# Attention scores in split precision: the second pass on half the rows of TensorE, two of them beside each other

## The chip, the cores and the metric

The kernel runs on one core of a Trainium2 chip. The metric is the device time of one execution in microseconds (us), as the median of several runs. Engines are called as in the profile: PE is TensorE's matmul, PEld its weight load, DVE VectorE, ACT ScalarE, POOL GpSimd, and SP SyncE, which here issues DMAs.

## What is computed

One layer of a hybrid encoder over 1024 prompt frames and 32 sample frames, all in float32: a combined projection, an attention branch and a convolution branch that are merged by gates, an output projection, an MLP, a gated embedding and norms. The change touches the attention of the prompt: 8 heads of width 64, 128 queries at a time, no softmax.

```python
def stick_breaking(q, k, v, q_pos, k_pos):
    scale = 1.0 / math.sqrt(HEAD_DIM)
    z = jnp.einsum('bqhd,bkhd->bhqk', q.astype(jnp.float32), k.astype(jnp.float32)) * scale
    mask = k_pos[None, :] < q_pos[:, None]
    log_1m = jnp.where(mask, jax.nn.log_sigmoid(-z), 0.0)
    tail = lax.cumsum(log_1m, axis=3, reverse=True) - log_1m
    a = jnp.where(mask, jnp.exp(jax.nn.log_sigmoid(z) + tail), 0.0)
    out = jnp.einsum('bhqk,bkhd->bqhd', a, v.astype(jnp.float32))
```

## The kernel before

Matmuls are done in split precision: a float32 operand becomes a high part in TensorE's rounded format and a low part, the rest; a product then takes two or three matmuls, high by high, high by low and low by high, added up in PSUM.

The attention is written as 64 steps (p, j, i): 4 pairs of heads (p), 2 heads in each (j), 8 query blocks (i). Step i looks at L = 128(i + 1) keys. The work of one step is spread over the program's next ones: `scores` in step n (matmuls into a PSUM tile z, a sigmoid on ACT into r, a causal select on POOL), `weigh` in step n+1 (a scan on DVE), `flip` in step n+2 (transposes pa on PE, cast on ACT and subtraction on DVE into at), and after each second block `gather` (the matmuls av against the values, which ACT and DVE take out and add). The string `ORDER = "LSAFBFG"` sets the order inside a step: scan, scores, transposes, fill (F), further transposes, fill, gather.

Fill is other work for PE, in units of a few hundred ns: the embedding projection (ps_pw, ps_pt) and the output of the convolution branch (ps_oc). `pace` spreads it: it estimates what the chain of a step needs (`load`) and what PE does for the step itself (`own`), and gives each step a share of the fill. The order on PE, DVE, ACT and POOL is the order in which the code is written; DMAs from SP stand in the order in which the tile framework schedules them.

A head is 64 wide, and PE's array has 128 rows. So the tile `kk` (ks in the profile) holds a head's high part of the keys in rows 0 to 63 and the low part in rows 64 to 127. The tile `q` has two versions of the queries: `q[:, 0]` with the high part above and the low part below, `q[:, 1]` the other way round. The first pass (L1206) gives high by high plus low by low, the second (L1207) the two mixed products, each for 128 queries and W keys. W is L up to 512 keys; from 640 keys on there are two z tiles of W = L/2 (320 to 512), one after the other. A pool of two PSUM buffers holds them.

`keys_values` fetches the keys and the values of a head by SP, eight steps before its step of index 2 (six before its first). All its tiles come from one pool of 37 blocks (`blk`), which other work uses too.

The 32 sample frames have an attention of their own in the same stretch (tiles zs, pas, avs). Its matmuls use parts of the array: zs (L1450) 64 rows and 32 columns, avs 128 rows and 64 columns (L1481) and 32 rows and 64 columns (L1483). The profile writes this as rows*columns.

Of the kernel before, what the change touches and what calls it, by code (L numbers as in the profile page):

```python
# [9 lines left out]
F32 = mybir.dt.float32  # L10
F32R = mybir.dt.float32r
# [4 lines left out]
P = 128  # L16
D = 1024
KD = D // P
SEQ = 1024
# [47 lines left out]
START = 0.33  # L67
BP = (8, 9)
TAIL = 0
FILL = 23.28 - START - TAIL  # L70
MM = {mybir.EngineType.Activation, mybir.EngineType.PE, mybir.EngineType.DVE, mybir.EngineType.Pool}

# [2 lines left out]
def tile_step(  # L75
# [8 lines left out]
    nc = tc.nc  # L84
# [7 lines left out]
    def blk(name, dt=F32, shape=None):  # L92
        return bpool.tile(shape or [P, T], dt, tag="B", name=name)
# [705 lines left out]
    kd = dpool.tile([4, 2, P, SEQ], F32, name="kd")  # L799
# [36 lines left out]
    st, cst = {}, {}  # L836
# [336 lines left out]
    def keys_values(p, j):  # L1173
        kk = st["k", p, j] = blk(f"ks{p}{j}", F32R, [P, SEQ])
        for i in range(2):
            nc.sync.dma_start(kk[64 * i : 64 * i + 64, :].bitcast(F32), kd[p, i, 64 * j : 64 * j + 64, :])
        vv = st["v", p, j] = blk(f"vv{p}{j}", F32R, [P, 8, P])
        nc.sync.dma_start(vv.bitcast(F32).rearrange("p a c -> p (a c)"), vd[p, j])

# [17 lines left out]
    def scores(p, j, i):  # L1197
        q, kk = live["q", p, j, i // 2], st["k", p, j]
        L = P * (i + 1)
        nh = 1 if L <= 512 else 2  # L1200
        W = L // nh
        tq = slice((i % 2) * P, (i % 2) * P + P)
        r = apool.tile([P, SEQ], F32, tag="R", name=f"r{p}{j}{i}", bufs=4)
        for h in range(nh):
            z, c = zps.tile([P, 512], F32, tag="z", name=f"z{p}{j}{i}{h}")[:, :W], slice(h * W, h * W + W)
            nc.tensor.matmul(z, q[:, 0, tq], kk[:, c], start=True, stop=False)  # L1206
            nc.tensor.matmul(z, q[:, 1, tq], kk[:, c], start=False, stop=True)  # L1207
            nc.scalar.activation(r[:, c], z, AF.Sigmoid, scale=-1.0)  # L1208
        earlier(r[:, L - P : L], 1.0)
        live[p, j, i] = (r, L)  # L1210

    def earlier(a, fill):

        n = a.shape[-1]
        nc.gpsimd.affine_select(  # L1215
            a, a, pattern=[[-1, n]], compare_op=ALU.is_gt, fill=fill, base=0, channel_multiplier=1
        )
# [170 lines left out]
    with tc.manual_schedule(engines=MM):  # L1388
# [17 lines left out]
        for a in range(3, last_, 2):  # L1406
# [4 lines left out]
            run(input_pair(a, a + 1))  # L1411
        m = blk(f"m1_i{last_}"), blk(f"m2_i{last_}")
        side.append(after(2, call(p_fetch), call(keys_values, 0, 0), call(queries, 0, 0, 0), call(queries, 0, 0, 1), call(queries, 0, 0, 2), call(queries, 0, 0, 3)))
        side.append(after(8, *(call(p_parts, f) for f in range(2)), *(call(embed_weights, i) for i in range(2))))
        side.append(after(9, call(next, work)))
# [9 lines left out]
    zps = c_att.enter_context(tc.tile_pool(name="zps", bufs=2, space=PSUM))  # L1425
# [63 lines left out]
    def pace():  # L1489

        ns = len(steps)

        def size(n):
            return steps[n][2] + 1 if 0 <= n < ns else 0

        load, own = [], []
        for n in range(ns + LAG):
            a, b, c = size(n - 1), size(n - LAG), size(n - LAG - 1)
            v = 0.29 * a + 0.17 * b + 0.35 + 0.42 * (c % 2 == 0 and c > 0)
            load.append(max(v, 1.6) + 3.0 * (n == 6 + 4) + 0.5 * (n == 4 + 4) + 0 * (n > 16 and n % 16 in BP))  # L1500
            own.append(0.24 * size(n) + 0.11 * b + 0.24 * c * (c % 2 == 0))
        for more in (None,):
            unit = (FILL * 2.92 + sum(own)) / sum(load)
            part = [max(0.0, unit * v - o) for v, o in zip(load, own)]
            part = [x * FILL / sum(part) for x in part]
            ends = [sum(part[: n + 1]) for n in range(ns + LAG)]
            if more is not None:
                load[next(n for n, e in enumerate(ends) if e > more)] += 0
        return ends

    sample = samples()
    nf = ORDER.count("F")
    pace_ = [0.0] + pace()
    with tc.manual_schedule(engines=MM):
        next(sample)
        for n in range(len(steps) + LAG + 1):
            done_f, parts = 0, None
            w0, w1 = (pace_ + [FILL])[n : n + 2]
            if n < len(steps):
                i = steps[n][2]  # L1520
                if i % 2 == 0 and 4 <= n < len(steps) - 4:
                    p_, j_, i_ = steps[n + 4]
                    queries(p_, j_, i_ // 2)
                if i == 2 and n + 8 < len(steps):
                    keys_values(*steps[n + 8][:2])
# [3 lines left out]
            for op in ORDER:  # L1529
                if op == "S" and n < len(steps):  # L1530
                    scores(*steps[n])
                elif op == "L":
                    if 1 <= n <= len(steps):
                        weigh(*steps[n - 1])
                    settle_owed()
                elif op == "F":
                    done_f += 1
                    fill(START + w0 + (w1 - w0) * done_f / nf)
                elif op == "G" and n > LAG and steps[n - LAG - 1][2] % 2 == 1:
                    p, j, i_ = steps[n - LAG - 1]  # L1540
                    gather(p, j, i_ // 2)
                elif op in "AB" and LAG <= n < len(steps) + LAG:
                    if op == "A":
                        parts = flip(*steps[n - LAG])
                    next(parts, None)
# [1010 lines left out]
```

## Time and profile before

| | |
|---|---|
| median of 3 runs | 1513.21 us (1512.92 to 1514.24) |
| span of the profiled execution | 1512.7 us |
| PE busy in the span | 1494.0 us (99%) |
| chain that ended last | PE 91%, DVE 5%, ACT 2%, issue 1%, DMA 1% |
| first to last score matmul | 430.8 to 600.0 us |
| DMA queue of SP and others (q1) | 260.44 MB, 51.0% of 16 engines |

The profile gives the span alone for its execution; the median of the runs is 0.5 us above it. The span runs from the first instruction recorded to the last. Matmul durations in the records overlap, since the array is filled by one while another drains; how far apart their starts or ends are says more than their length. The chain of waits follows the work that ended last back through what released each instruction, so the time beside an entry is what it added.

### The profile page before, as it was taken

What the parts mean: (1) busy time and instruction counts of PE and PEld (TensorE: products, weight loads), DVE (VectorE), ACT (ScalarE), POOL (GpSimd) and SP (SyncE); (2) the same over time, 40 slices, a digit from 0 to 9 for tenths busy, and PEclk for the clock granted to TensorE, in tenths of its full rate; (3) what the DMA queues carried; (4) which work ended last, traced back from release to release, by engine and by line L of the source; (5) the groups of instructions that cost most, each with busy time, mean ns of one, the idle gap of its engine ahead of it and who ended that gap; (6) DMA issues with size and microseconds to landing.
All of it is one profiled execution on the core that took longest, in us unless ns stands there. A gap on an engine that the chain in (4) does not pass through costs nothing.

```text
span 1512.7 us, 29442 instructions
## 1 busy us (share of the span) xinstructions
PE 1494.0 (99%) x11552; PEld 1479.0 (98%) x11552; DVE 1152.1 (76%) x1624; ACT 791.1 (52%) x1567; POOL 376.1 (25%) x334
## 2 busy tenths in 40 slices
PE   8999999999999999999999999999999999999997
PEld 8999999999999999999999999999999999999997
DVE  7667689779668999886786676666688878879766
ACT  6654444444467667433475545555555433334655
POOL 1234335444121232003324434333000000000251
PEclk9999999999999999999999999999999999999999
DMA  6624424422679676654644334444879757855443
GB/s 231 207 90 170 148 69 182 158 93 100 211 249 284 178 172 139 228 199 152 231 166 147 139 136 156 157 150 157 303 287 279 255 185 231 301 189 165 142 129 123
DMA packets 116747, 275.52 MB, mean 182 GB/s; under 512 B 14048, under 2 KB 30048, under 8 KB 116608
## 3 DMA queue, kind: packets, MB, share of 16 engines
q1 hardware_dynamic: 112720, 260.44, 51.0%
q0 software_dynamic: 1728, 6.29, 2.5%
q10 hardware_dynamic: 2160, 6.91, 1.4%
q8 instruction: 91, 1.49, 0.4%
q14 instruction: 48, 0.39, 0.1%
HBM read 196.10 MB, written 85.88 MB: 186 GB/s over the span
## 4 chain that ended last, share of the span: by engine, by line
PE 91%; DVE 5%; ACT 2%; issue 1%; DMA 1%; SPq 0%; ACTq 0%; DVEq 0%
PE ps_dn L1996 6%; PE ps_dn L1995 6%; PE ps_dn L1994 6%; PE ps_A11i L370 4%; PE ps_A11u L371 4%; PE ps_A11i L371 4%; PE ps_A11u L370 4%; PE ps_A11u L372 4%; PE ps_A11i L372 4%; PE av L1277 3%; PE ps_wo L132 2%; PE ps_wo L133 2%; PE ps_wo L134 2%; PE ps_S1i L372 2%; PE ps_S1i L371 2%; PE ps_S1i L370 2%
## 5 line engine op out<-in xcount | busy, mean ns | idle before, releaser
L1996 PE MATMUL ps_dn<-fhP,wlo_dn 128*128 128x264 f32 x768 | 218.6, 285 | 0.0
L1995 PE MATMUL ps_dn<-flP,whi_dn 128*128 128x264 f32 x768 | 218.2, 284 | 0.2 <-DVE flP L1860 0.2
L1994 PE MATMUL ps_dn<-fhP,whi_dn 128*128 128x264 f32 x768 | 218.3, 284 | 0.0
L1995 PEld LDWEIGHTS ps_dn<-flP,whi_dn 128*128 128x128 f32 x768 | 144.5, 188 | 0.4 <-DVE flP L1860 0.4
L1996 PEld LDWEIGHTS ps_dn<-fhP,wlo_dn 128*128 128x128 f32 x768 | 144.5, 188 | 0.2 <-DVE wlo_dn L1844 0.2
L1994 PEld LDWEIGHTS ps_dn<-fhP,whi_dn 128*128 128x128 f32 x768 | 144.5, 188 | 0.0
L1222 DVE TENSOR_TENSOR_SCAN r<-r 128x128 f32<-128x128 f32 (+3 forms) x64 | 86.7, 1355 | 5.3 <-POOL r L1215 5.3
L2209 POOL TENSOR_TENSOR xx<-xx,pgs 128x400 f32<-128x400 f32 (+1 forms) x17 | 20.1, 1184 | 280.9 <-DVE pgs L2208 280.9
L370 PE MATMUL ps_A11i<-T,shS_i 128*128 128x264 f32 x288 | 82.7, 287 | 1.0 <-ACT u_i L514 1.0
L372 PE MATMUL ps_A11i<-T,slS_i 128*128 128x264 f32 x288 | 81.8, 284 | 0.5 <-DVE slS_i L249 0.5
L371 PE MATMUL ps_A11i<-T,shS_i 128*128 128x264 f32 x288 | 82.1, 285 | 0.0
L370 PE MATMUL ps_A11u<-T,shS_u 128*128 128x264 f32 x256 | 73.3, 286 | 0.0
L371 PE MATMUL ps_A11u<-T,shS_u 128*128 128x264 f32 x256 | 73.0, 285 | 0.0
L372 PE MATMUL ps_A11u<-T,slS_u 128*128 128x264 f32 x256 | 72.7, 284 | 0.0
L1215 POOL TENSOR_SCALAR_AFFINE_SELECT r<-r 128x128 f32<-128x128 f32 x64 | 35.7, 559 | 131.9 <-ACT r L1208 131.8
L1838 ACT CAST whi_dn<-raw_dn 128x1024 fp32r<-128x1024 f32 x31 | 32.6, 1051 | 64.8 <-PE ps_dn L1995 52.7
L1860 DVE TENSOR_TENSOR flP<-mrP,fhP 128x1056 fp32r<-128x1056 f32 x48 | 59.9, 1250 | 4.9 <-ACT fhP L1855 4.8
L134 PE MATMUL ps_wo<-mh,wlo_wo 128*128 128x352 f32 x192 | 62.0, 323 | 0.0
L133 PE MATMUL ps_wo<-ml,whi_wo 128*128 128x352 f32 x192 | 62.0, 323 | 0.0
L132 PE MATMUL ps_wo<-mh,whi_wo 128*128 128x352 f32 x192 | 61.7, 324 | 0.0
L249 DVE TENSOR_TENSOR slS_i<-s_i,shS_i 128x512 fp32r<-128x512 f32 x54 | 48.9, 905 | 12.7 <-ACT shS_i L190 12.4
L1262 DVE TENSOR_TENSOR at<-pa,at 128x512 fp32r<-128x512 f32 (+2 forms) x96 | 50.4, 547 | 9.4 <-ACT at L1261 8.6
(1702 smaller groups left out, 5793.1 us busy)
## 6 DMA issues: line engine op xcount, KB each, us to landing
raw_dn<-in_w_down_dram SPq DMA_DIRECT2D x59, 512.0 KB, 5.6
mrP<-mdT SPq DMA_DIRECT2D x32, 528.0 KB, 5.8
mdB<-m SPq DMA_DIRECT2D x48, 264.0 KB, 2.1
mrP<-mdB SPq DMA_DIRECT2D x24, 528.0 KB, 6.6
s<-gd SPq DMA_DIRECT2D x16, 528.0 KB, 5.3
mdT<-ta SPq DMA_DIRECT2D x32, 264.0 KB, 3.1
raw_pg<-in_w_ple_gate_dram SPq DMA_DIRECT2D x15, 512.0 KB, 3.5
gd<-m_i SPq DMA_DIRECT2D x12, 528.0 KB, 3.0
```

What stands on the lines that cost most here:

```text
L132: nc.tensor.matmul(ps, wh, xh[k][:, cols], start=(k == order[0]), stop=False)
L133: nc.tensor.matmul(ps, wh, xl[k][:, cols], start=False, stop=False)
L134: nc.tensor.matmul(ps, wl, xh[k][:, cols], start=False, stop=(k == order[-1]))
L370: nc.tensor.matmul(p_, wh[:, k, :], h, start=new and n == 0, stop=False, **on)
L371: nc.tensor.matmul(p_, wh[:, k, :], l, start=False, stop=False, **on)
L372: nc.tensor.matmul(p_, wl[:, k, :], h, start=False, stop=z, **on)
L1222: nc.vector.tensor_tensor_scan(rev, rev, rev, 1.0, ALU.mult, ALU.bypass)
L1262: nc.vector.tensor_tensor(al, pt[:, :nb, :], ah.bitcast(F32), op=ALU.subtract)
L1860: dve(l, mraw.pop(v), opd[v].bitcast(F32), op=sub)
L1994: nc.tensor.matmul(ps, hi[:, j, :], oh, start=j == 0, stop=False)
L1995: nc.tensor.matmul(ps, hi[:, j, :], ol, start=False, stop=False)
L1996: nc.tensor.matmul(ps, lo[:, j, :], oh, start=False, stop=j == NP_ - 1)
```

## The change

- `keys_values` writes the high part of the keys into both halves of `kk`, and a second tile `kl` (`low`) gets the low part: keys 0 to 511 in rows 0 to 63, keys 320 to 1023 in rows 64 to 127. That is two DMAs more for each head.
- `scores` makes one pass with all 128 rows for each z tile: `q[:, 0]` against the high part twice gives high by high plus low by high. Then comes one pass with 64 rows for each z tile, the high part of the queries against the low part of the keys. From 640 keys on there are two of these, the first in rows 0 to 63, the second in rows 64 to 127, on different rows and into different z tiles. The product of the two low parts is no longer computed.
- Steps with up to 512 keys have one pass with 128 rows and one with rows 0 to 63.
- Both z tiles are taken before the first sigmoid; the sigmoids stand behind all matmuls of the step.
- `pace` gives steps with 640 keys and more a smaller `own`.

```diff
+FAR = 320
...
         for i in range(2):
-            nc.sync.dma_start(kk[64 * i : 64 * i + 64, :].bitcast(F32), kd[p, i, 64 * j : 64 * j + 64, :])
+            nc.sync.dma_start(kk[64 * i : 64 * i + 64, :].bitcast(F32), kd[p, 0, 64 * j : 64 * j + 64, :])
+        low = st["l", p, j] = blk(f"kl{p}{j}", F32R, [P, SEQ - FAR])
+        for i, c in enumerate((slice(0, SEQ // 2), slice(FAR, SEQ))):
+            nc.sync.dma_start(
+                low[64 * i : 64 * i + 64, : c.stop - c.start].bitcast(F32), kd[p, 1, 64 * j : 64 * j + 64, c]
+            )
...
-        for h in range(nh):
-            z, c = zps.tile([P, 512], F32, tag="z", name=f"z{p}{j}{i}{h}")[:, :W], slice(h * W, h * W + W)
-            nc.tensor.matmul(z, q[:, 0, tq], kk[:, c], start=True, stop=False)
-            nc.tensor.matmul(z, q[:, 1, tq], kk[:, c], start=False, stop=True)
+        low = st["l", p, j]
+        zs_, cs_ = [], [slice(h * W, h * W + W) for h in range(nh)]
+        for h, c in enumerate(cs_):
+            zs_.append(zps.tile([P, 512], F32, tag="z", name=f"z{p}{j}{i}{h}")[:, :W])
+            nc.tensor.matmul(zs_[h], q[:, 0, tq], kk[:, c], start=True, stop=False)
+        for h, c in enumerate(cs_):
+            rows_, n0 = slice(64 * h, 64 * h + 64), c.start - h * FAR
+            nc.tensor.matmul(zs_[h], q[rows_, h, tq], low[rows_, n0 : n0 + W], start=False, stop=True)
+        for z, c in zip(zs_, cs_):
             nc.scalar.activation(r[:, c], z, AF.Sigmoid, scale=-1.0)
...
-            own.append(0.24 * size(n) + 0.11 * b + 0.24 * c * (c % 2 == 0))
+            own.append((0.24 - 0.028 * (size(n) > 4)) * size(n) + 0.11 * b + 0.24 * c * (c % 2 == 0))
```

Two places show what it does to the order. On PE, in the first head, from the transposes (pa) of the step with 512 keys to those of the next, which has 640; z are the two score tiles, ps_pw is fill. Before:

```order
L1258 MATMUL pa_5652<-ident,r_5598 128x128 x2
L1134 MATMUL ps_pw_5657<-p0h,pw0h 128x352
L1135 MATMUL ps_pw_5657<-p0l,pw0h 128x352
L1136 MATMUL ps_pw_5657<-p0h,pw0l 128x352
L1134 MATMUL ps_pw_5657<-p1h,pw0h 128x352
L1135 MATMUL ps_pw_5657<-p1l,pw0h 128x352
L1136 MATMUL ps_pw_5657<-p1h,pw0l 128x352
L1206 MATMUL z_5672<-ks_5348,q_5407 128x320
L1207 MATMUL z_5672<-ks_5348,q_5407 128x320
L1206 MATMUL z_5676<-ks_5348,q_5407 128x320
L1207 MATMUL z_5676<-ks_5348,q_5407 128x320
L1258 MATMUL pa_5685<-ident,r_5621 128x128 x3
```

On PE at the same place after the change (kl are the low halves, 64 rows each; the lines are those of the changed kernel):

```order
L1269 MATMUL pa_5658<-ident,r_5601 128x128 x2
L1214 MATMUL z_5669<-ks_5348,q_5410 128x320
L1214 MATMUL z_5671<-ks_5348,q_5410 128x320
L1217 MATMUL z_5669<-kl_5351,q_5410 128x320
L1217 MATMUL z_5671<-kl_5351,q_5410 128x320
L1269 MATMUL pa_5682<-ident,r_5627 128x128 x3
L1135 MATMUL ps_pw_5688<-p0h,pw0h 128x352
L1136 MATMUL ps_pw_5688<-p0l,pw0h 128x352
```

The two passes against ks now stand together, the two against kl behind them, and a block of six fill matmuls has moved from ahead of the scores to behind the transposes.

On SP, the loads of the third head's keys and values (q are queries, ed an output of the fill). Before:

```order
L1169 DMA q_5980<-qd 64x2x256
L1170 DMA q_5980<-qd 64x256
L1171 DMA q_5980<-qd 64x256
L1176 DMA ks_5984<-kd 64x1024 x2
L1178 DMA vv_5987<-vd 128x1024
L1139 DMA ed<-em_5964 128x1056
```

On SP after the change:

```order
L1171 DMA q_5986<-qd 64x256
L1172 DMA q_5986<-qd 64x256
L1177 DMA ks_5990<-kd 64x1024 x2
L1180 DMA kl_5993<-kd 64x512
L1180 DMA kl_5993<-kd 64x704
L1184 DMA vv_5996<-vd 128x1024
L1140 DMA ed<-em_5970 128x1056
```

The two loads of kl stand between the high halves and the values; what follows keeps its order.

## The prediction

> **What bounds the kernel now.** First the page: TensorE is busy from end to end at the full granted clock. Then the stretch that the edit touches, the 64 attention steps, by the view of windows (us, then busy time and count of each engine, granted clock, DMA share, GB/s).
>
> ```profile
> PE 1494.0 (99%) x11552; PEld 1479.0 (98%) x11552; DVE 1152.1 (76%) x1624; ACT 791.1 (52%) x1567; POOL 376.1 (25%) x334
> PEclk9999999999999999999999999999999999999999
> ...
> 430.60:601.20 170.60, 168.58 (x1215) 159.16 (x1214) 147.49 (x201) 122.92 (x322) 45.26 (x87) 1.00 0.75 207
> ```
>
> TensorE has 2 us of gaps in 170.6; VectorE is busy 147.5 and has 23 to spare. So time that TensorE gains or loses here moves the end, unless it falls into one of its few waits. The waits of this stretch, TensorE's (and its weight loader's) alone (us in total, times, the longest):
>
> ```profile
> PEld pa L1258 <- PE z L1207: 1.5, 4, 0.4
> PEld av L1277 <- DVE at L1262: 1.4, 3, 0.5
> PEld z L1206 <- ACT r L1208: 0.9, 2, 0.5
> PE av L1277 <- DVE at L1262: 0.8, 3, 0.3
> PEld avs L1481 <- issue: 0.4, 2, 0.3
> PE z L1206 <- ACT r L1208: 0.4, 2, 0.2
> ```
>
> The first, second and fourth (3.7 us, at three or four places) are the handovers between heads, where VectorE and ScalarE are late. Busy times of matmuls overlap, so what a pass costs I read from the chain of waits, in order of time (start, time added, what), where each matmul adds only what it lengthens:
>
> ```profile
> 171.15 0.11 PE pts_v L923
> 171.26 0.12 PE ps_A11i L370
> ...
> 446.67 1.00 PE zs L1450 x16
> 447.67 0.26 PE z L1206
> 447.92 0.11 PE z L1207
> ...
> 455.38 0.18 PE z L1207
> ...
> 461.92 0.15 PE z L1207
> ...
> 468.67 0.93 PE av L1277 x8
> 469.61 0.36 PE avs L1481 x8
> 469.97 0.23 PE avs L1483 x4
> 470.20 0.43 PE z L1206
> 470.63 0.23 PE z L1207
> ...
> 472.91 0.18 PE ps_pw L1136
> ...
> 532.17 0.21 PE z L1207
> ```
>
> A score pass over 320, 384, 448 and 512 keys adds 0.15, 0.18, 0.21 and 0.23 us. And the row that decides this case: at 470.20 the same 512-key pass adds 0.43. It stands behind matmuls on part of the array (L1483). Their shapes, and when the weights go in, from the timeline (start, duration, rows*columns of the array in use):
>
> ```profile
> 472.75 0.35 PE L1136 MATMUL ps_pw<-p1h,pw1l 128*128 128x400 f32 x1
> ...
> 473.03 0.32 PEld L1481 LDWEIGHTS avs<-ats,cv 128*64 128x64 f32 x8 [0.27 <-issue]
> ...
> 470.13 0.19 PEld L1206 LDWEIGHTS z<-ks,q 128*128 128x128 f32 x1
> 470.24 0.19 PEld L1207 LDWEIGHTS z<-ks,q 128*128 128x128 f32 x1
> ...
> 446.60 1.07 PE L1450 MATMUL zs<-kk,qs 64*32 64x288 f32 x16
> ...
> 170.99 0.27 PE L923 MATMUL pts_v<-ident,m_i 128*32 128x128 f32 x1
> ```
>
> Elsewhere a weight load starts with the matmul before it and is hidden. At 473.03 it starts 0.28 after the start of a 400-column pass that adds 0.18 (472.91), having waited for nothing that the profile shows: TensorE first ran empty (0.10). At 470.13 the load of 128 columns stands open too: the next load, which goes with the start of the first real streaming, is 0.11 later. Going from one division of the array to another thus costs an emptying of 0.10 and an open load of 0.11, about 0.20; 0.43 - 0.23 says the same.
>
> **The change, part by part.** Each of the 64 steps now has one shape change in and one out: full 128-row passes against the key high halves, then passes on 64 rows and 128 columns against the low halves, then the transposes on the whole array.
>
> *Shape changes, 128 of them.* No row shows a 64*128 division, so the price is bounded. From below: the 128*32 transposes of L923 between full passes add 0.11, and the pass behind them its usual 0.12: no pause, price 0. From above: 0.26, all that the short 128-key pass at 447.67 adds behind a change. I take 0.20 (0.43 - 0.23), since every half of a pair here ends in a 128-column load behind another division, as that row does. 128 x 0.20 = +25.6; the bounds are 0 and 33.3.
>
> The row and a rule: the Trainium skill, TensorEngine Tiling (Array Packing), section Key Properties, says that changing the tiling mode, not merely the tile, drains the engine. The trace agrees at L1481 and at the return to L1206. Its section Restrictions and Gotchas lists transposes as incompatible with column tiling, by which the unpaused transposes would be no change of mode; no run here shows why they pass. By that rule the sum is the one with 0.20; without it the passes saved are all that is left.
>
> *Passes saved.* In the 32 long steps two passes lie side by side in place of two in a row: per head 0.15 + 0.18 + 0.21 + 0.23 = 0.77, times 8 = -6.2. That 64-row passes run side by side the trace shows: the 16 of L1450, 288 columns each, take 1.00 together, where one after the other, at the 0.12 of the 264-column pass at 171.26, they would take 1.9 at the least. A late start of the second, 0.01 x 32, +0.3 (an estimate: 14 weight loads of that group follow one another within 0.1).
>
> *Steps of 128 keys.* There a pass adds 0.11 (447.92), the load's time and not the streaming's, so an open load replaces something: about -0.1 x 8 = -0.8. The short steps otherwise save nothing: still two passes, and two shape changes.
>
> *What the waits swallow.* At three handovers (502, 545, 588 us) the chain runs through ScalarE and VectorE while TensorE does the steps of 256 and 384 keys and then waits:
>
> ```profile
> 585.83 0.35 ACT avl L1288
> 586.18 0.53 ACT o2h L1294
> ...
> 588.36 0.70 DVE at L1262
> ...
> 589.10 2.03 PE av L1277 x15
> ```
>
> Four shape changes, 0.8, fall into each: 3 x 0.8 = -2.4, of the 3.7 that is there to swallow (bounds 0 and 3.7).
>
> *The score buffers.* There are two; both halves are now asked for before either is read. The step of 640 keys therefore wants the second after one full pass, 0.15 earlier than before, but the change out of the step ahead takes 0.20 first. The waits on r (0.9 + 0.4) stay as they are: 0, bounds -0.4 and +1.2 (0.15 x 8). The first half's sigmoid begins up to two passes later; its result is scanned a step and flipped two steps later, so that is hidden. If it weren't, those waits on r would grow first.
>
> *Keys laid out twice.* Two more DMAs for each head, 311 KB, on SP; one issue takes about 0.6 and lands in 5.7 (from the view of tile ks: min/median/max):
>
> ```profile
> L1176 SPq DMA_DIRECT2D ks<-kd x16: 445/594/1497, 405.9 to 561.3; - x16
> DMA to landing us min/median/max: 3.5/5.7/9.5
> ...
> 436.77 1.82 SPq L1176 DMA_DIRECT2D ks<-kd x2
> 438.64 0.85 SPq L1178 DMA_DIRECT2D vv<-vd x1
> ...
> 447.60 0.33 PE L1206 MATMUL z<-ks,q 128*128 128x128 f32 x1
> ```
>
> The low halves of the second head would be issued by 439.8 and land near 445.5, with the first use after 447.6; the values and queries behind them on SP come 1.2 later with several us to spare. Cost 0; at the slowest landing (9.5) 1.7 once, which the slower steps ahead would cover. Two more blocks in flight may make a load wait for an older block; the loads run six steps ahead, so 0 again.
>
> *The planner's smaller cost.* Fill matmuls are placed by it; six blocks of six move past a neighbour, none is added. 0, bounds -0.5 and +0.5.
>
> Sum: 25.6 - 6.2 + 0.3 - 0.8 - 2.4 = +16.5. On the profiled execution's span of 1512.7 that gives 1529.2; the runs' median, 1513.2, is 0.5 above the span, so 1529.7.
>
> **The rivals.**
> *A, faster: no pause between 128 and 64 rows.* Both are full in columns, and the transposes show that a narrower shape alone need not pause. Then -6.2 + 0.3 is left: 1507.3. Against it: L1481 to L1483 keep their columns and change rows alone, and the four matmuls of L1483 add 0.23, as if a pause were in them. It decides where a change costs under 0.05 (128 x 0.05 = 6.4). The Trainium skill, TensorEngine Tiling (Array Packing), section Theoretical Speedup, allows up to 2x for contractions of 64 rows, which read alone is this case. Chance 0.11.
> *B, the half-row passes don't overlap,* since both write all 128 partitions of the accumulator, and the change doesn't do what it says: +6.2 on the sum, 1535.9. L1450 speaks against it (two row halves onto the same partitions), though there in narrow columns. Chance 0.08.
> *C, only one direction pays,* the load going ahead in the other: 64 x 0.20 - 6.2 + 0.3 - 0.8 - 1.2 = +4.9, 1518.1. Chance 0.11.
> *D, a change costs next to 0.05* and cancels the gain: 1513. Chance 0.02.
>
> **The numbers.** The forecast has 0.68; its own range, with prices of 0.16 to 0.24 and the swallowed part from 0 to 3.7, is 1523 to 1538 (at 0.16: 5 less; at 0.24: 5 more; the waits 1 to 2 either way). At the upper bound of 0.26 it would be 1537. With C and B the range 1516 to 1540 leaves out A, D and some tails, about 2 in 10. About 0.2% (3 us) is what a measurement here can tell: faster 0.11 (A), same 0.02 (D), slower 0.87.
>
> **What would show it.** In the changed trace: the low-half weight loads starting 0.1 after the high pass has streamed, not with its start; the first transpose behind a score step late by 0.2; in long steps the two low passes starting within 0.02 of each other; TensorE's records in this stretch spread over about 187 us; VectorE's busy time unchanged at 147. Wrong would be loads that start with the pass before them (A), low passes a whole pass apart (B), a pause on one side alone (C), or a score step that waits for kl.

## The result, and the profile after

The changed kernel takes 1527.24 us (median of 4 runs, 1526.85 to 1527.29) beside 1513.15 (4 runs, 1512.92 to 1514.24): a ratio of 1.009, interval 1.0079 to 1.0102, slower by 14.1. The forecast was 1529.5 (the prediction's own sum ends at 1529.7), the range 1516 to 1540.

The page of the changed kernel, busy times and granted clock:

```profile
PE 1507.3 (99%) x11552; PEld 1472.8 (97%) x11552; DVE 1152.8 (76%) x1624; ACT 795.9 (52%) x1567; POOL 370.5 (24%) x334
...
PEclk9999999999999999999999999999999999999999
```

TensorE has as many instructions as before and the same clock, and its busy time is 13.3 longer; that of VectorE is 0.7 longer. The weight loads are 6 shorter in sum, but what counts of a load is whether it stands open. Now the windows (us, busy time and count of each engine, granted clock, DMA share, GB/s): of the changed kernel from the first score matmul to the last sigmoid of the scores, and on to the first matmul of the output projection, then of the kernel before over the second of these stretches:

```profile
429.00:613.20 184.20, 182.92 (x1218) 153.51 (x1218) 150.01 (x201) 127.73 (x323) 40.04 (x86) 1.00 0.73 205
429.00:624.07 195.07, 193.79 (x1297) 164.31 (x1297) 157.58 (x212) 133.50 (x337) 41.35 (x88) 1.00 0.74 210
```

```profile
430.76:612.66 181.90, 179.88 (x1298) 170.37 (x1297) 155.81 (x212) 128.97 (x337) 47.47 (x88) 1.00 0.76 209
```

The stretch from the first score to the output projection, called the stage from here on, is 13.2 longer (195.07 - 181.90); with the same work, TensorE's busy time grew by 13.9 (193.79 - 179.88). Its idle time fell from 2.0 to 1.3. So nothing new is waited for: the matmuls themselves are farther apart. The stage and the medians are the measures to go by. The spans differ by 12.8 only, since the profiled execution of the kernel before started its stage 1.8 later than the other one; and 1.4 more comes behind the stage, 1.3 of it in the MLP's last projection (ps_dn), which the change doesn't touch.

Why the matmuls are farther apart, in the timeline of the changed kernel, in the step of the fifth head with 1024 keys (start, duration, rows*columns of the array in use):

```profile
542.45 0.40 PE L1214 MATMUL z<-ks,q 128*128 128x512 f32 x1
542.77 0.19 PEld L1217 LDWEIGHTS z<-kl,q 64*128 64x128 f32 x2 [0.36 <-issue]
542.77 0.50 PE L1217 MATMUL z<-kl,q 64*128 64x512 f32 x2
543.20 0.14 PEld L1269 LDWEIGHTS pa<-ident,r 128*128 128x128 f32 x1 [0.24 <-issue]
543.20 0.33 PE L1269 MATMUL pa<-ident,r 128*128 128x128 f32 x1
543.26 0.14 PEld L1269 LDWEIGHTS pa<-ident,r 128*128 128x128 f32 x1
```

The last full pass starts at 542.45. The weights of the half-row pass go in at 542.77, 0.32 later, though a pass of 512 adds 0.23: TensorE ran empty for 0.09, having waited for nothing else. Both half-row passes then cover one and the same time (x2, 0.50 for the pair; in the records the second starts 3 to 4 ns behind the first). At 543.20 the same again on the way out, ahead of the transposes. What that adds up to is in the chain (start, time added, what), of the changed kernel, in two places:

```profile
472.33 0.66 PE z L1214 x2
473.00 0.42 PE z L1217
473.42 0.81 PE pa L1269 x6
...
475.94 0.26 PE z L1214
476.19 0.25 PE z L1217
476.45 0.59 PE pa L1269 x4
...
538.98 0.41 PE z L1214 x2
539.40 0.40 PE z L1217 x2
539.80 0.59 PE pa L1269 x4
...
542.38 0.46 PE z L1214 x2
542.84 0.42 PE z L1217
```

and in that of the kernel before:

```profile
467.03 0.55 PE pa L1258 x5
...
473.95 0.11 PE z L1207
474.06 0.46 PE pa L1258 x4
```

In: the half-row pass of 512 keys adds 0.42 where a full pass added 0.23, so 0.19 more; the prediction had 0.20. Out: a transpose adds 0.11 (0.55 for five), four of them 0.44, six 0.66; behind the half-row passes they add 0.59 and 0.81, 0.15 more. The prediction took 0.20 for that too. The reason is in the records at 543.20: the next transpose's load follows 0.06 after the first (543.26), where behind an open load of a score the next followed after 0.11 (470.13 and 470.24 in the kernel before). A transpose's load lasts 0.14, a score's 0.18 to 0.19. So a pair of changes costs 0.34, not 0.40. Step by step the records say the same: from a step's first score load to the third load behind its passes, and with the saved pass put back in long steps, the two kernels differ by 0.34 to 0.35 in the median for each length from 256 to 1024 keys. The step of 128 keys pays 0.25 - 0.11 = 0.14 on the way in and 0.59 - 0.46 = 0.13 on the way out; its pair costs 0.27. The Trainium skill, TensorEngine Tiling (Array Packing), section Key Properties, says that a change of the tiling mode drains TensorE; the trace agrees for 64*128, with 0.09 empty ahead of each load.

TensorE's waits in the stage, of the changed kernel (us in total, times, the longest):

```profile
PEld z L1217 <- issue: 12.6, 49, 0.4
PEld pa L1269 <- issue: 9.3, 45, 0.2
...
PEld av L1288 <- DVE at L1273: 1.6, 4, 0.4
PEld z L1214 <- ACT r L1219: 1.2, 3, 0.4
PE av L1288 <- DVE at L1273: 0.7, 3, 0.2
PE z L1214 <- ACT r L1219: 0.5, 3, 0.2
```

The first two rows are new: it is the loader standing idle until the array is empty, and they are the mark of a shape change, not its price (the array still streams for most of that time). The wait of the transposes (1.5 before) is gone, and those of av on VectorE stand at 1.6 + 0.7, where they were 1.4 + 0.8; the waits on r grew by 0.4. No row names a load of kl, or any other DMA.

At three handovers between heads TensorE's waits swallow some of the pairs. The step of 384 keys in the fourth head, from its first score load to the load that waits for VectorE, in the kernel before and in the changed one:

```profile
501.92 0.19 PEld L1206 LDWEIGHTS z<-ks,q 128*128 128x128 f32 x1
...
503.68 0.19 PEld L1277 LDWEIGHTS av<-at,vv 128*128 128x128 f32 x1 [0.47 <-DVE at L1262]
```

```profile
506.68 0.19 PEld L1214 LDWEIGHTS z<-ks,q 128*128 128x128 f32 x1
...
508.12 0.19 PEld L1288 LDWEIGHTS av<-at,vv 128*128 128x128 f32 x1 [0.44 <-DVE at L1273]
```

This took 1.76 and takes 1.44, so 0.32 less, where the same step of each of the first three heads takes 0.34 more. So 0.66 is swallowed here, as much as two pairs. The sixth and the eighth head show the same, with 0.35 and 0.34 less.

### The profile page after: what moved, and what is told of

Same layout as the page of the kernel before. It is cut to its first block, busy times and chain, and to the rows that moved or that the text cites. A ratio compares the mean times of both kernels' runs of the same rounds, so it can differ in the third digit from the quotient of the medians.

```text
span 1525.5 us, 29486 instructions
## 1 busy us (share of the span) xinstructions
PE 1507.3 (99%) x11552; PEld 1472.8 (97%) x11552; DVE 1152.8 (76%) x1624; ACT 795.9 (52%) x1567; POOL 370.5 (24%) x334
## 4 chain that ended last, share of the span: by engine, by line
PE 91%; DVE 4%; ACT 2%; DMA 2%; issue 1%; SPq 0%; ACTq 0%; DVEq 0%
PE ps_dn L2007 6%; PE ps_dn L2006 6%; PE ps_dn L2005 6%; PE ps_A11i L371 4%; PE ps_A11i L372 4%; PE ps_A11i L373 4%; PE ps_A11u L371 4%; PE ps_A11u L372 4%; PE ps_A11u L373 4%; PE av L1288 2%; PE pa L1269 2%; PE ps_S1i L373 2%; PE ps_S1i L372 2%; PE ps_S1i L371 2%; PE ps_wo L133 2%; PE ps_wo L135 2%
## 5 line engine op out<-in xcount | busy, mean ns | idle before, releaser
L1226 POOL TENSOR_SCALAR_AFFINE_SELECT r<-r 128x128 f32<-128x128 f32 x64 | 29.5, 461 | 150.7 <-ACT r L1219 146.9
```

## The experiments

In what was expected, S is the theory that the shape changes make the time, with a price for each pair. All numbers on the stage are from the profiled execution, as above (before 181.90); all times are medians, with the ratio to the kernel before on the same chip (1512.51 for the first four, 1512.72 for the others). In the first four and in the seventh kl holds all 1024 keys in both halves, 524 KB for each head instead of 311.

| kernel | us | ratio | stage, against before |
|---|---|---|---|
| changed kernel | 1527.24 | 1.009 (1.0079 to 1.0102) | +13.2 |
| all passes on 128 rows | 1518.41 | 1.0035 (1.0023 to 1.0048) | +3.8 |
| half rows in long steps only | 1520.77 | 1.0061 (1.0048 to 1.0074) | +8.0 |
| half rows in short steps only | 1522.71 | 1.0073 (1.0060 to 1.0087) | +8.4 |
| both half passes on the same rows | 1533.29 | 1.0137 (1.0123 to 1.0151) | +19.1 |
| order alone | 1513.47 | 1.0004 (0.9995 to 1.0013) | +1.0 |
| loads alone | 1515.09 | 1.0018 (1.0009 to 1.0027) | +0.9 |
| short steps in pairs | 1522.14 | 1.0062 (1.0050 to 1.0075) | +11.7 |
| one by one | 1543.10 | 1.0200 (1.0186 to 1.0214) | +30.0 |

**All passes on 128 rows.** The changed kernel's layout, order and planner, but no shape change: the second pass is again full.

```diff
-            nc.tensor.matmul(zs_[h], q[rows_, h, tq], low[rows_, n0 : n0 + W], start=False, stop=True)
+            nc.tensor.matmul(zs_[h], q[:, 1, tq], low[:, c], start=False, stop=True)
```

> The changed kernel with its key layout, its order of passes, its delayed sigmoids and its planner number, but every second pass on all 128 rows (both halves of kl hold the whole low part), so that no step changes the division of the array. Theory S (the shape changes cost the time, about 0.20 in and 0.15 out, less 6 us for the passes saved): 1512 to 1514.5, as before the change. Rival W (the two score buffers asked for together, the later sigmoids, the added DMAs and the moved fill cost it): 1523 to 1527. Rival H (the passes on 64 rows run slowly or not side by side): 1512 to 1514.5, as S.

Measured: 1518.41, a miss: 5.9 slower without any shape change. In the profile 3.2 of the stage's 3.8 come in the first two heads, and the chain shows most of it at one place, the first step of the third head:

```profile
466.55 7.62 DMA q<-qd
474.17 0.14 issue
474.31 0.30 PE z L1212
```

TensorE waits for queries; in the list of waits of the same kernel this reads

```profile
PE z L1212 <- DMA q<-qd: 1.9, 1, 1.9
```

It isn't kl that is late but what stands behind it on SP. The issues there, from the keys of the third head to its first queries (start, duration), in this kernel:

```profile
454.96 2.40 SPq L1177 DMA_DIRECT2D ks<-kd x2
458.79 1.88 SPq L1180 DMA_DIRECT2D kl<-kd x2
462.77 0.33 SPq L1182 DMA_DIRECT2D vv<-vd x1
...
465.96 0.54 SPq L1170 DMA_DIRECT2D q<-qd x1
```

and in the changed kernel:

```profile
456.07 1.23 SPq L1177 DMA_DIRECT2D ks<-kd x2
457.40 1.18 SPq L1180 DMA_DIRECT2D kl<-kd x2
459.14 0.33 SPq L1184 DMA_DIRECT2D vv<-vd x1
...
461.46 0.59 SPq L1170 DMA_DIRECT2D q<-qd x1
```

From the keys to the queries it takes SP 11.0 here and 5.4 there (7.7 in the kernel before). SP's own waits in this kernel name transfers of cv (4.7 in all, at kl, the values and the keys), which hold blocks of the same pool; in the changed kernel they are 0.5 at the values. So this price of the larger kl is real, and the changed kernel's profile has no such wait.

**Half rows in long steps only, and in short steps only.** From the kernel above, two halves of the change:

```diff
+            if nh == 2:
+                nc.tensor.matmul(zs_[h], q[rows_, h, tq], low[rows_, c], start=False, stop=True)
+            else:
+                nc.tensor.matmul(zs_[h], q[:, 1, tq], low[:, c], start=False, stop=True)
```

(the second kernel has `nh == 1`).

> As the run with all rows, but in the 32 steps with 640 keys and more the second pass is two passes on 64 rows side by side; the short steps have no shape change. Theory S: 32 pairs of changes at 0.33 to 0.36, +10.6 to 11.5, less 6.2 saved: 1517 to 1519. Rival H: nearly all of the loss sits here, 1524 to 1528. Rival W: 1523 to 1527.

> As the run with all rows, but in the 32 steps with up to 512 keys the second pass uses rows 0 to 63 alone; the long steps have no shape change. No pass is saved, so this is the price of 32 pairs of changes by itself. Theory S: +10.6 to 11.5, less 0.8 in the 128-key steps and 1 to 2 swallowed at the handovers between heads: 1520.5 to 1523. Rival H: a pass on 64 rows that stands alone costs little, 1513 to 1515.

Measured: 1520.77, above what was expected, as the kernel with all passes on 128 rows was. Both profiled executions have the wait for queries (1.9 there, 1.6 here), so their stages compare: 4.2 longer. 32 pairs less the 6.2 of passes saved make that, (4.2 + 6.2)/32 = 0.32 for a pair; by the medians, 2.4 apart, it would be 0.27. The short steps: 1522.71, as expected. Against the kernel with full passes their stage grows by 4.6 only, but in heads 1 and 2 by -0.4 (its profile has no wait for queries; that its slower steps give them the time is argued, not shown); over heads 3 to 8 it is 5.0, 0.21 for each of the 24 pairs, net of what the handovers and the steps of 128 keys give back. So long steps don't pay either: a pair costs 0.32 there, net, and a step saves 0.15 to 0.23.

**Both half passes on the same rows.** The second pass of a long step uses rows 0 to 63 for both tiles, so the two can't lie side by side; nothing else differs but the size of kl.

```diff
-            nc.tensor.matmul(zs_[h], q[rows_, h, tq], low[rows_, n0 : n0 + W], start=False, stop=True)
+            nc.tensor.matmul(zs_[h], q[0:64, 0, tq], low[0:64, c], start=False, stop=True)
```

> As the changed kernel, but in the long steps both passes on 64 rows use rows 0 to 63, so that they can't lie side by side. Theory S: the 6.2 us saved are given back, 1532.5 to 1534. Rival H (they don't lie side by side in the changed kernel either): 1527, as the changed kernel.

Measured: 1533.29, 20.8 over the kernel before on its chip, where the changed kernel was 14.1 over: 6.7 more. The stage is 5.97 longer, between 0.71 and 0.79 in each of the 8 heads (0.77 was worked out for the four passes). In its chain, steps of 768 and 1024 keys:

```profile
540.47 0.55 PE z L1214 x2
541.01 0.59 PE pa L1266 x4
...
546.65 0.66 PE z L1214 x2
547.30 0.59 PE pa L1266 x4
```

The two half passes of 512 add 0.66 = 0.23 + 0.23 + 0.20, where they added 0.42 side by side. The way out stays at 0.59 for four transposes. So rival B is refuted, and the term of passes saved is shown.

**Order alone.** The kernel before with the changed order of passes, both buffers taken first, late sigmoids and the planner's number; keys, loads and passes as before.

```diff
-            nc.tensor.matmul(z, q[:, 0, tq], kk[:, c], start=True, stop=False)
-            nc.tensor.matmul(z, q[:, 1, tq], kk[:, c], start=False, stop=True)
...
+            nc.tensor.matmul(zs_[h], q[:, 0, tq], kk[:, c], start=True, stop=False)
+        for h, c in enumerate(cs_):
+            nc.tensor.matmul(zs_[h], q[:, 1, tq], kk[:, c], start=False, stop=True)
```

> The kernel before (its key layout, its loads, four passes on 128 rows in a long step) with the changed order inside the step (both z tiles first, sigmoids behind all passes) and the changed planner number. It asks where the run with all rows lost its 6 us. Theory L (the added loads come late for the next head): 1512 to 1514, as before. Theory W (waits on the two score buffers and the later sigmoids): 1516 to 1519.

Measured: 1513.47, no difference that can be told (its interval reaches from -0.8 to +2.0 us).

**Loads alone.** The kernel before with the two loads of kl for each head, which nothing reads.

```diff
+        low = st["l", p, j] = blk(f"kl{p}{j}", F32R, [P, SEQ - 320])
+        for i, c in enumerate((slice(0, SEQ // 2), slice(320, SEQ))):
+            nc.sync.dma_start(
+                low[64 * i : 64 * i + 64, : c.stop - c.start].bitcast(F32), kd[p, 1, 64 * j : 64 * j + 64, c]
+            )
```

> The kernel before with the two loads of the low halves added in each head, which nothing reads; passes, order and planner as before. Theory L: 1515 to 1518, lost in the first two heads, where a score step waits for a query load. Theory W: 1512 to 1514.

Measured: 1515.09, 2.4 slower, with single runs from 1513.32 to 1518.66, where those of the changed kernel lie within 0.5. The profiled execution was among the faster ones and shows 0.9 in the stage, all of it in the first head, and one wait of 0.4 for queries. That is what theory L said, at its lower end. So the loads have a price, which differs from run to run, where no slower step covers it.

**Short steps in pairs.** Two neighbouring steps up to 512 keys have their scores made together, with their half passes side by side: 48 pairs of changes instead of 64.

```diff
+        if i < 4 and i % 2:
+            return
+        if i < 4:
+            parts_ = [(i + u, slice(0, P * (i + u + 1)), slice(u * P, u * P + P)) for u in range(2)]
...
+        for h, (i_, c, tq) in enumerate(parts_):
+            rows_ = slice(64 * h, 64 * h + 64)
+            nc.tensor.matmul(zs_[h], q[rows_, h, tq], low[rows_, c], start=False, stop=True)
```

> The changed kernel, but the scores of two short steps (128 and 256 keys, 384 and 512) are made together in the earlier step: two passes on all rows, then the two passes on 64 rows side by side. 48 pairs of shape changes are left of 64, and in each short pair a pass is saved. Theory S at 0.33 a pair: 16 x 0.33 = 5.3 and 8 x (0.11 + 0.18) = 2.3 less than the changed kernel, 1519.5 to 1521, up to 2 more where waits at the head's start come out again. If the number of shape changes doesn't set the time: 1525 to 1528.

Measured: 1522.14, 9.4 over the kernel before, so 4.7 less than the changed kernel was. That is above the 1519.5 to 1521 that was expected, and inside the 2 more that was allowed for waits; single runs reach from 1518.89 to 1525.33, and the profiled one is the slowest of them. It again has a wait for queries, at the first step of a head:

```profile
PE z L1216 <- DMA q<-qd: 2.7, 2, 2.5
```

That the time falls with 16 pairs fewer (and some passes beside each other) is shown; the price of one can't be had from the times, since the profile taken is one with 2.5 of waiting in it. Its records have it all the same: in the joined steps of 384 and 512 keys the loads of the half passes start 0.49 to 0.50 after the load of the second full pass, 0.08 to 0.09 more than the two full passes add (0.18 + 0.23), and the transposes' load follows 0.42 to 0.43 later, as in the changed kernel.

**One by one.** In long steps each tile has its full pass and then its half pass, so 96 pairs and no overlap.

```diff
             nc.tensor.matmul(zs_[h], q[:, 0, tq], kk[:, c], start=True, stop=False)
-        for h, c in enumerate(cs_):
             rows_, n0 = slice(64 * h, 64 * h + 64), c.start - h * FAR
```

> The changed kernel, but in the long steps each z tile has its pass on all rows and its pass on 64 rows before the next: 96 pairs of shape changes instead of 64, and nothing side by side. Theory S: 32 x (0.19 + 0.20) = 12.5 (here a 128-row load stands open on the way back, 0.11 instead of the transpose's shorter one) and 6.2 given back, 1545 to 1547. If a pair costs less than 0.2 where nothing waits for it: below 1540.

Measured: 1543.10, 30.4 over the kernel before, 16.3 more than the changed kernel was, and less than expected; the stage is 16.9 longer than the changed kernel's. Less the 6.2 of overlap given up, the 32 pairs added cost 10.7, 0.33 each, with what the waits swallow taken off. The chain has such a step of 640 keys:

```profile
542.23 0.15 PE z L1214
542.38 0.34 PE z L1216
542.72 0.34 PE z L1214
543.06 0.34 PE z L1216
543.40 0.48 PE pa L1268 x3
```

A pass of 320 adds 0.15; each one behind a change adds 0.34, the full pass behind a half pass too. So the way out costs 0.19 where a score pass comes next, and 0.15 (0.48 - 0.33) where a transpose does: the price goes with the load that has to stand open.

## Why the prediction was right, and where not

The forecast was 2.3 high, its sum +16.5 for +14.1. Point by point:

- **Shape changes, +25.6: mis-sized.** The mechanism is shown on both sides: the changed kernel's timeline, and the runs that take away, halve and add changes. Rivals A and D have no case left, and C neither, since both directions cost. The step that failed is "since every half of a pair here ends in a 128-column load behind another division, as that row does": the way out ends in a transpose's load, which is shorter (0.14 beside 0.19) and stands open for 0.06, not 0.11. 64 x (0.19 + 0.15) = 21.8.
- **Passes saved, -6.2: right.** With both passes on the same rows the stage gives 6.0 of it back. The late start of the second pass is 0.004, 0.1 in all instead of 0.3.
- **128-key steps, -0.8: most of it.** A pair costs 0.27 there instead of 0.34, part of it saved on the way in and part on the way out: 8 x 0.07 = -0.6.
- **Swallowed at the handovers, -2.4: nearly right.** Two pairs fall into each handover, as the prediction had it, at the smaller price: the fourth, sixth and eighth heads give 3 x (0.34 + 0.33) = -2.0. The rows of waits are no measure of it: they fell from 3.7 to 2.3 only, and the 3.7 has the waits of av twice, for the loader and for TensorE itself. In the chain of the changed kernel a handover still runs through ScalarE and VectorE. Another 0.3 was swallowed where the prediction expected nothing, at the end of the first head: the sample frames' scores (zs) had waited for VectorE in two rows of 0.2 that are gone. In the chain they add 0.65 now, so the 1.00 that the prediction read for them held a wait.
- **Score buffers, 0:** the waits on r grew from 1.3 to 1.7, three of them instead of two: +0.4, inside the bounds.
- **Keys laid out twice, 0, hidden by the slower steps: right in the changed kernel, not by itself.** TensorE's waits name no load there. The loads alone cost 2.4, and 5.9 came with larger ones and the new order, not through kl but through the queries behind it on SP, for which the prediction had "several us to spare", and through waits for blocks, which it put at 0. That the slower steps are the cover is argued from the issues on SP and the waits; the short-step kernel, where heads 1 and 2 take no more time than with full passes, speaks for it.
- **Planner, 0: right** (order alone, +0.8 with an interval from -0.8 to +2.0), though in the traces nine blocks of six fill matmuls stand on the other side of a step's scores, not six.

With the measured sizes: 21.8 - 6.2 + 0.1 - 0.6 - 2.0 - 0.3 + 0.4 = 13.2, which is what the stage grew by in the profile; other waits of 0.3 that came and went in the fifth and seventh heads cancel. The 0.9 by which the medians differ more than the stage does stays open. Behind the stage every other profile is longer than that of the kernel before, by 0.1 to 1.4, those without shape changes too (order alone 0.6, loads alone 0.7); what makes it was not tried. That the forecast's sum came within 2.4 of the medians is in part luck: the price of the changes was 3.8 too high, of which the other terms took back 0.5, and the 0.9 from outside the stage had no term at all. Of what the prediction said would be seen, the starts of the loads (0.1 late), the two half passes together, and VectorE came (150.0, predicted 147); the stretch is 184 and not 187, and the transposes are late by 0.15, not 0.2.

None of the versions run beats the kernel before.

## What to carry to other kernels

Count the changes of the array's division before counting the passes saved: here a pair costs 0.34 us, and a half-row pass saves only the streaming of its partner, 0.23 for 512 columns, so a pair pays from about 760 saved columns on (0.34/0.23 x 512, an estimate; no kernel here had the score buffers for it). What a change costs is the emptying plus as much of the next weight load as stands open, so look at which load comes behind it. And an added load is free only as long as what queues behind it on the same DMA queue is not the next thing that TensorE needs: try it alone, and with the steps as fast as they are to become.

## What the runs showed of the hardware that was not expected

- Behind the same change a transpose's weight load stands open for 0.06 and a score pass's for 0.11; the emptying is 0.09 in both.
- Two half-row passes of up to 512 columns, both with 128 columns of the array and into different PSUM tiles, start 3 to 4 ns apart (all 32 pairs of the changed kernel), and together last as long as one: with 512 columns the next load follows after 0.42 to 0.43, behind one alone and behind two.
- A kernel with nothing but two unread loads more for each head spread over 5.3 us from run to run (1513.32 to 1518.66), where the order alone spread over 1.8 and the kernel before, in 20 runs on the same chip, over 2.6.
